# One wide matmul in place of two in a channel-major fp32 projection of a two-layer decoder trunk

## The chip, the core and the metric

The kernel runs on one core of a Trainium2 chip. The metric is device microseconds (us) of one execution; before the change the median of three runs is 497.79 us (497.72 to 498.26). A profiled execution gives the trace that is read below. PE is TensorE's matmul side, PEld its weight load, DVE VectorE, ACT ScalarE, POOL GpSimd, SP SyncE, which issues the weight loads.

## The reference

Two pre-norm residual layers over 256 tokens of 1024 channels, all in float32. Layer 0 mixes tokens by attention, layer 1 by causal pooling; each is followed by a squared-ReLU MLP of width 4096, and a last RMS norm ends the program. Cut to what matters here:

```python
# layer 0 (256 tokens are one block: plain causal attention, 8 heads of 128)
qkv = rms_norm(x, norm_mix[0]) @ w_qkv
q, k = rope(q), rope(k)                 # the first 32 channels of each head are rotated
x = x + softmax(causal(q @ k.T / sqrt(128))) @ v @ w_o
# both layers
h = relu(rms_norm(x, norm_mlp[l]) @ w_up[l])
x = x + (h * h) @ w_down[l]
```

## The kernel before

**Split operands.** A product of float32 values is made of products of float32r values. Each weight slab (1 MB: 128 partitions x 2048 elements) is loaded to a `raw` buffer by SP, ScalarE copies it to a high part `wh` (L160), and VectorE subtracts to get the low part `wl` (L164), in two pieces of 128x1024 (four for the first slabs). Activations are split likewise: `xs[:, k, 0:256]` is the high part of channel tile `k`, `xs[:, k, 256:512]` the low part. A product takes three passes, high x high, low weight x high, high weight x low.

**Channel-major products** (queries, keys, up-projection): the weights stand still, the activations move, and the result has channels on partitions and 256 tokens on the free axis. `chan_block` (L368) computes one half `f` (128 channels) of a slab: for each of eight channel tiles `k` three matmuls of 256 columns, at L360 (`wh` x high), L361 (`wl` x high) and L365 (`wh` x low). Both halves of a slab lie in one PSUM bank `u`, from a pool of two (`ps_u`), so a slab takes 48 matmuls. **Token-major products** (values, output projection, down-projection) move the weights and take three matmuls of 512 columns (L351 to L353).

**Order.** All engines run an order written out by hand: each executes its instructions in the order in which the code issues them. `pump(n)` issues the next n pieces of the weight split (a `wh` on ScalarE, a `wl` on VectorE), at most three slabs (`AHEAD`) ahead of the slab in use; `pump_h` and `pump_l` issue the halves of a piece apart. The split's last `wl` piece of a slab also issues a later slab's load on SP.

**Queries and keys** (loop at L571): for each of four head pairs `j`, the key slab, then the scores of the pair before, then the query slab, then the transposes of the probabilities of the pair before. `qk_evac` (L495) turns a bank into rotated keys or queries: VectorE shuffles 32 rows to `sw` (L500) and multiplies the bank by a cosine table into the tile `t` (L501); POOL multiplies `sw` by a sine table (L502) and adds it to `t` (L503). `scores` (L510) takes `t_k` and `t_q`: score matmuls into `s` (L517, L518), row maxima on VectorE (L521, negated at L525), exponentials with their sums on ScalarE (L530), reciprocal of the sums (L533) and scaling of the probabilities `p` (L537) on VectorE. `prob_t` transposes `p` on TensorE (L548).

**MLP** (`mlp`, L667): per step `i`, the up slab `u_i`, then the down slab of step `i - 2`; steps 0 to 2 have no down slab in front, so three up slabs stand in a row. `up_evac` (L641): ScalarE takes relu out of the bank (L646), VectorE squares it to `hf` (L647), ScalarE squares it to the high part `hh` (L648), VectorE subtracts to `hl` (L649). `first_up` (L652) computes slab 0 of a layer with the last transposes of the residual (`tr_m`, L287) in the middle of it; ScalarE (L293) and VectorE (L299) make the two parts of `xs` from them.

Of the kernel before, what the change touches and what calls it, by code (L numbers as in the profile page):

```python
# [83 lines left out]
def tile_trunk(ctx: ExitStack, tc: tile.TileContext, x_in, positions, norm_mix, norm_mlp,  # L84
# [237 lines left out]
    def rsqrt_steps(acc, s, nm):  # L322
        """1 / sqrt(variance + eps), in three steps: VectorE, ScalarE, VectorE."""
# [25 lines left out]
    def tok_mm(acc, lh, ll, wh, wl, first, last):  # L349
        """Three passes of a token-major product: hi*hi + hi*lo + lo*hi."""  # L350
# [4 lines left out]
    def chan_hi(acc, w, k, f, first):  # L355
        """Channel-major product with the activations' high part: two of the three passes."""
# [15 lines left out]

    def d_banks(nm):
# [18 lines left out]
    def rotary():  # L392
        """Angles reduced to one turn."""
# [83 lines left out]
    # rstd along the free axis, folded with the rotary tables  # L477
# [32 lines left out]
    def scores(j):  # L510
# [60 lines left out]
    for j in range(4):  # L571
        w = use("k", j)
        u = qk_bank("k", j)
        chan_block(u, w, 0)
# [8 lines left out]
        chan_block(u, w, 1)  # L583
# [3 lines left out]
        qk["k", j] = qk_evac("k", j, u)  # L587
# [53 lines left out]
    def up_evac(l, i, u):  # L641
        r = work.tile([P, HALF], F32, tag="Z", name="relu_%d_%d" % (l, i), bufs=4)
# [292 lines left out]
```

## Time and profile before

| what | value |
|---|---|
| median of three runs | 497.79 us |
| profiled execution, first to last instruction | 496.7 us |
| PE busy | 485.3 us (98%) |
| PEld busy | 442.2 us (89%) |
| DVE busy | 304.7 us (61%) |
| ACT busy | 245.7 us (49%) |
| POOL busy | 50.1 us (10%) |
| granted TensorE clock, mean | 0.996 |

The profiled execution's own time is its span, 496.7 us; the runs' median lies 1.1 us above it, which is what stands around the first and the last instruction. Busy times of an engine count each instruction from start to end, and matmuls overlap: the pace of TensorE is read from the starts of matmuls that follow each other, not from their durations.

### The profile page before, as it was taken

How to read it: one execution, taken by the hardware profiler on the slowest of the kernel's cores; microseconds unless marked ns; L12 is line 12 of the kernel's file. 1: busy time of each engine (PE TensorE's matmuls, PEld its weight loads, DVE VectorE, ACT ScalarE, POOL GpSimd, SP SyncE). 2: the span in 40 equal slices, each digit the busy share in tenths (PEclk: the TensorE clock that was granted, in tenths of full speed). 3: DMA queues.
4: the chain of work that ended last, by engine and by line, in shares of the span. 5: the costliest groups of instructions: out<-in, count | busy, mean ns of one | idle time of the engine just before them, and what ended most of it. 6: DMA issues, size and time to landing. Idle time of an engine off the chain costs nothing.

```text
span 496.7 us, 7616 instructions
## 1 busy us (share of the span) xinstructions
PE 485.3 (98%) x3137; PEld 442.2 (89%) x3137; DVE 304.7 (61%) x420; ACT 245.7 (49%) x363; POOL 50.1 (10%) x46
## 2 busy tenths in 40 slices
PE   9999999999999999999999999999999999999993
PEld 7789899889999999999999989999999999999982
DVE  3788788765858555555565576676455555544435
ACT  4776444554766444444444443584444444444423
POOL 6936524200000000000000000000000000000000
PEclk9999999999999999999999999999999999999998
DMA  7959525570596556555444660188555555666002
GB/s 269 385 167 282 167 87 169 157 246 22 180 360 192 193 203 211 207 194 170 170 170 173 187 234 1 52 260 295 192 177 170 169 172 184 200 204 230 29 0 84
DMA packets 56081, 89.59 MB, mean 180 GB/s; under 512 B 1600, under 2 KB 44640, under 8 KB 56048
## 3 DMA queue, kind: packets, MB, share of 16 engines
q1 hardware_dynamic: 55632, 88.68, 53.2%
q8 instruction: 24, 0.39, 0.3%
q10 hardware_dynamic: 352, 0.41, 0.2%
q14 instruction: 9, 0.07, 0.0%
q0 software_dynamic: 64, 0.03, 0.0%
HBM read 88.06 MB, written 1.05 MB: 179 GB/s over the span
## 4 chain that ended last, share of the span: by engine, by line
PE 88%; POOL 5%; DVE 2%; issue 2%; ACT 1%; DMA 1%; POOLq 0%; DVEq 0%; ACTq 0%
PE u_m L365 12%; PE u_m L361 12%; PE u_m L360 12%; PE d_m L353 12%; PE d_m L352 12%; PE d_m L351 12%; POOL rot_b L403 2%; PE d_o L353 1%; PE d_o L351 1%; PE d_o L352 1%; PE u_q L365 1%; PE u_q L360 1%; PE u_q L361 1%; PE pb L781 1%; DMA raw_k<-in_attn_w_qkv_dram 1%
## 5 line engine op out<-in xcount | busy, mean ns | idle before, releaser
L361 PE MATMUL u_m<-xs,wl_u 128*128 128x256 f32 x512 | 144.1, 283 | 0.0
L360 PE MATMUL u_m<-xs,wh_u 128*128 128x256 f32 x512 | 143.0, 281 | 0.0
L365 PE MATMUL u_m<-xs,wh_u 128*128 128x256 f32 x512 | 141.9, 285 | 0.0
L353 PE MATMUL d_m<-wh_d,hl 128*128 128x512 f32 x256 | 100.1, 391 | 0.0
L352 PE MATMUL d_m<-wl_d,hh 128*128 128x512 f32 x256 | 100.1, 391 | 0.0
L351 PE MATMUL d_m<-wh_d,hh 128*128 128x512 f32 x256 | 99.8, 390 | 0.0
L360 PEld LDWEIGHTS u_m<-xs,wh_u 128*128 128x128 f32 x512 | 97.0, 189 | 1.0
L361 PEld LDWEIGHTS u_m<-xs,wl_u 128*128 128x128 f32 x512 | 96.3, 188 | 1.0
L646 ACT ACTIVATE relu<-u_m 128x512 f32<-128x512 f32 x32 | 19.1, 597 | 157.2 <-PE u_m L365 157.2
L647 DVE TENSOR_TENSOR hf<-relu 128x512 f32<-128x512 f32 x32 | 22.1, 692 | 121.1 <-ACT relu L646 121.1
L365 PEld LDWEIGHTS u_m<-xs,wh_u 128*128 128x128 f32 x512 | 95.0, 189 | 0.0
L164 DVE TENSOR_TENSOR wl_d<-raw_d,wh_d 128x1024 fp32r<-128x1024 f32 x64 | 77.6, 1222 | 8.6 <-ACT wh_d L160 5.0
L164 DVE TENSOR_TENSOR wl_u<-raw_u,wh_u 128x1024 fp32r<-128x1024 f32 x64 | 75.3, 1219 | 1.7 <-ACT wh_u L160 1.5
L160 ACT ACTIVATE wh_d<-raw_d 128x1024 fp32r<-128x1024 f32 x64 | 66.1, 1045 | 6.7 <-DMA raw_d<-in_mlp_w_down_dram 6.7
L160 ACT ACTIVATE wh_u<-raw_u 128x1024 fp32r<-128x1024 f32 x64 | 63.7, 1045 | 0.0
L353 PEld LDWEIGHTS d_m<-wh_d,hl 128*128 128x128 f32 x256 | 48.0, 188 | 10.1
L352 PEld LDWEIGHTS d_m<-wl_d,hh 128*128 128x128 f32 x256 | 48.0, 188 | 9.5
L351 PEld LDWEIGHTS d_m<-wh_d,hh 128*128 128x128 f32 x256 | 48.1, 188 | 9.3
L649 DVE TENSOR_TENSOR hl<-hf,hh 128x512 fp32r<-128x512 f32 x32 | 22.2, 693 | 3.3
L648 ACT ACTIVATE hh<-relu 128x512 fp32r<-128x512 f32 x32 | 20.3, 634 | 1.1
L360 PE MATMUL u_q<-xs,wh_q 128*128 128x256 f32 x64 | 18.6, 290 | 0.0
L360 PE MATMUL u_k<-xs,wh_k 128*128 128x256 f32 x64 | 18.4, 288 | 0.0
(171 smaller groups left out, 595.2 us busy)
## 6 DMA issues: line engine op xcount, KB each, us to landing
raw_u<-in_mlp_w_up_dram SPq DMA_DIRECT2D x32, 1024.0 KB, 5.7
raw_d<-in_mlp_w_down_dram SPq DMA_DIRECT2D x32, 1024.0 KB, 6.7
raw_k<-in_attn_w_qkv_dram SPq DMA_DIRECT2D x4, 1024.0 KB, 5.4
raw_q<-in_attn_w_qkv_dram SPq DMA_DIRECT2D x4, 1024.0 KB, 5.3
raw_o<-in_attn_w_o_dram SPq DMA_DIRECT2D x4, 1024.0 KB, 5.1
raw_v<-in_attn_w_qkv_dram SPq DMA_DIRECT2D x3, 1024.0 KB, 9.7
raw_v<-in_attn_w_qkv_dram SPq DMA_DIRECT2D x4, 256.0 KB, 4.1
pw<-in_pool_w_dram SPq DMA_DIRECT2D x1, 1024.0 KB, 10.9
```

The source lines that it names most:

```text
L160: nc.scalar.activation(wh[:, sl], src[:, sl], AF.Copy)
L164: nc.vector.tensor_tensor(wl[:, sl], src[:, sl], wh[:, sl].bitcast(F32), op=ALU.subtract)
L351: nc.tensor.matmul(acc, lh, wh, start=first, stop=False)
L352: nc.tensor.matmul(acc, lh, wl, start=False, stop=False)
L353: nc.tensor.matmul(acc, ll, wh, start=False, stop=last)
L360: nc.tensor.matmul(o, w[0][:, k, fs], hi, start=first, stop=False, skip_group_check=True)
L361: nc.tensor.matmul(o, w[1][:, k, fs], hi, start=False, stop=False, skip_group_check=True)
L365: nc.tensor.matmul(acc[:, f * SEQ:(f + 1) * SEQ], w[0][:, k, fs], xs[:, k, SEQ:2 * SEQ], start=False, stop=last, skip_group_check=True)
L646: nc.scalar.activation(r, u, AF.Relu)
L647: nc.vector.tensor_tensor(hf, r, r, op=ALU.mult)
L648: nc.scalar.activation(hh, r, AF.Square)
L649: nc.vector.tensor_tensor(hl, hf, hh.bitcast(F32), op=ALU.subtract)
```

## The change

Three edits.

1. In the up-projection and in queries and keys, the high weights meet both activation parts in one matmul of 512 columns, since the two parts lie side by side in `xs`. Per `k` and `f` there are now two matmuls: `wl` x high (256 columns, L377 of the changed kernel) and `wh` x high and low (512 columns, L379), in this order. The result fills a whole bank per half slab: columns 0 to 255 hold two passes, columns 256 to 511 the third.
2. The two parts of the bank are added afterwards: ScalarE copies columns 256 to 511 to a tile `t`, VectorE adds columns 0 to 255 to it, for each half (L518 and L519 for queries and keys, L670 and L671 for the MLP). Rotation and squared ReLU then start from `t` in SBUF instead of the bank: `hf` is max(t, 0) x t in one VectorE instruction (L680), and `hh` a copy of `hf` on ScalarE (L681). For `j` = 0 the banks of queries and keys come from `ps_u`, for later pairs from the four banks (`ps_d`) that hold the values' sums before.
3. The scaling of the probabilities moves from VectorE (L537) to ScalarE (L564).

```diff
+    def wide_k(acc, w, k, f, first, last):
+        fs = slice(f * P, (f + 1) * P)
+        nc.tensor.matmul(acc[:, 0:SEQ], w[1][:, k, fs], xs[:, k, 0:SEQ],
+                         start=first, stop=False, skip_group_check=True)
+        nc.tensor.matmul(acc, w[0][:, k, fs], xs[:, k, :],
+                         start=False, stop=last, skip_group_check=True)
+
+    def wide_block(acc, w, f):
+        for k in range(KT):
+            wide_k(acc, w, k, f, k == 0, k == KT - 1)
+
+    def wide_bank(nm, i, f):
+        return ps_u.tile([P, HALF], F32, tag="u", name="u_%s_%d_%d" % (nm, i, f))
...
+    def qk_wide(nm, j, w, f, t):
+        if j == 0:
+            u = wide_bank(nm, j, f)
+        else:
+            u = ps_d.tile([P, HALF], F32, tag="d%d%d" % ("kq".index(nm), f), name="u_%s_%d_%d" % (nm, j, f))
+        wide_block(u, w, f)
+        nc.scalar.activation(t[:, f, :], u[:, SEQ:2 * SEQ], AF.Copy)
+        nc.vector.tensor_tensor(t[:, f, :], u[:, 0:SEQ], t[:, f, :], op=ALU.add)
...
-        nc.vector.stream_shuffle(sw.rearrange("p f t -> p (f t)"), u[0:ROT, :], swap)
-        nc.vector.tensor_tensor(t, uv, ct.broadcast_to([P, 2, SEQ]), op=ALU.mult)
+        nc.vector.stream_shuffle(sw.rearrange("p f t -> p (f t)"), t[0:ROT].rearrange("p f t -> p (f t)"), swap)
+        nc.vector.tensor_tensor(t, t, ct.broadcast_to([P, 2, SEQ]), op=ALU.mult)
...
-                nc.vector.tensor_scalar(pr[a][:, c0:c1], pr[a][:, c0:c1], sums[:, i:i + 1], None,
-                                        op0=ALU.mult)
+                nc.scalar.activation(pr[a][:, c0:c1], pr[a][:, c0:c1], AF.Copy, scale=sums[:, i:i + 1])
...
     for j in range(4):
         w = use("k", j)
-        u = qk_bank("k", j)
-        chan_block(u, w, 0)
+        t = qk_tile("k", j)
+        qk_wide("k", j, w, 0, t)
...
+    def up_sum(t, u, f):
+        ts = slice(f * SEQ, (f + 1) * SEQ)
+        nc.scalar.activation(t[:, ts], u[:, SEQ:2 * SEQ], AF.Copy)
+        nc.vector.tensor_tensor(t[:, ts], u[:, 0:SEQ], t[:, ts], op=ALU.add)
...
-        nc.scalar.activation(r, u, AF.Relu)
-        nc.vector.tensor_tensor(hf, r, r, op=ALU.mult)
-        nc.scalar.activation(hh, r, AF.Square)
+        nc.vector.scalar_tensor_tensor(hf, t, 0.0, t, op0=ALU.max, op1=ALU.mult)
+        nc.scalar.activation(hh, hf, AF.Copy)
...
-        u = qk_bank(nm, 0)
+        us = [wide_bank(nm, 0, f) for f in range(2)]
         for k0 in range(0, KT, 2):
             for f in range(2):
                 for k in (k0, k0 + 1):
-                    chan_hi(u, w, k, f, k == 0 and f == 0)
+                    wide_k(us[f], w, k, f, k == 0, k == KT - 1)
+                if f == 0 and k0 < 4:
+                    ev = transposes(k0 + 4, gbase, nm)
             if k0 < 4:
-                both(transposes(k0 + 4, gbase, nm, upool=k0 == 0))
-            for f in range(2):
-                for k in (k0, k0 + 1):
-                    chan_lo(u, w, k, f, k == KT - 1)
-        return up_evac(l, 0, u)
+                both(ev)
+        t = up_tile(l, 0)
+        for f in range(2):
+            up_sum(t, us[f], f)
+        return up_evac(l, 0, t)
...
-                u = qk_bank("m%d" % l, i)
-                chan_block(u, w, 0)
+                t = up_tile(l, i)
+                u = wide_bank("m%d" % l, i, 0)
+                wide_block(u, w, 0)
+                up_sum(t, u, 0)
                 pump(1)
-                chan_block(u, w, 1)
-                hid[i] = up_evac(l, i, u)
+                u = wide_bank("m%d" % l, i, 1)
+                wide_block(u, w, 1)
+                up_sum(t, u, 1)
+                hid[i] = up_evac(l, i, t)
                 pump(2)
```

How this moves instructions, at the three places of which the prediction speaks.

VectorE at the first head pair, before: the shuffle (L500) and the product (L501) of the keys and of the queries, with pieces of the split (L164) between them.

```order
L164 TENSOR_TENSOR wl_q_373<-raw_q_282,wh_q_372 128x1024
L164 TENSOR_TENSOR wl_k_420<-raw_k_348,wh_k_419 128x1024
L500 STREAM_SHUFFLE sw_k_452<-u_k_390 32x512
L501 TENSOR_TENSOR t_k_451<-u_k_390,ct_k 128x512
L164 TENSOR_TENSOR wl_k_420<-raw_k_348,wh_k_419 128x1024
L164 TENSOR_TENSOR wl_q_462<-raw_q_353,wh_q_461 128x1024 x2
L500 STREAM_SHUFFLE sw_q_519<-u_q_465 32x512
```

And of the change, the same stretch: the additions (L519) stand between the pieces.

```order
L519 TENSOR_TENSOR t_k_390<-u_k_0_391,t_k_390 128x256
L164 TENSOR_TENSOR wl_q_373<-raw_q_282,wh_q_372 128x1024
L164 TENSOR_TENSOR wl_k_415<-raw_k_348,wh_k_414 128x1024
L519 TENSOR_TENSOR t_k_390<-u_k_1_420,t_k_390 128x256
L527 STREAM_SHUFFLE sw_k_441<-t_k_390 32x512
L528 TENSOR_TENSOR t_k_390<-t_k_390,ct_k 128x512
L164 TENSOR_TENSOR wl_k_415<-raw_k_348,wh_k_414 128x1024
L164 TENSOR_TENSOR wl_q_451<-raw_q_353,wh_q_450 128x1024
L519 TENSOR_TENSOR t_q_454<-u_q_0_455,t_q_454 128x256
L164 TENSOR_TENSOR wl_q_451<-raw_q_353,wh_q_450 128x1024
L519 TENSOR_TENSOR t_q_454<-u_q_1_478,t_q_454 128x256
L527 STREAM_SHUFFLE sw_q_497<-t_q_454 32x512
```

Four additions stand ahead of the queries' shuffle that were not there, and shuffle and product now read `t`, which the last addition writes.

TensorE at the first up slab of layer 1, before, behind the last transposes of the residual (`tr_d`): the passes with the activations' high part first, the four with the low part (L365) behind the transposes `tr_m`.

```order
L287 MATMUL tr_d_2980<-ident,xt 128x128 x4
L360 MATMUL u_m_0_2990<-xs,wh_u_0_2778 128x256
L361 MATMUL u_m_0_2990<-xs,wl_u_0_2779 128x256
...
L287 MATMUL tr_m_4_2999<-ident,xt 128x128 x4
L365 MATMUL u_m_0_2990<-xs,wh_u_0_2778 128x256 x4
```

And of the change:

```order
L287 MATMUL tr_d_2700<-ident,xt 128x128 x4
L377 MATMUL u_m_0_0_2710<-xs,wl_u_0_2499 128x256
L379 MATMUL u_m_0_0_2710<-xs,wh_u_0_2498 128x512
L377 MATMUL u_m_0_0_2710<-xs,wl_u_0_2499 128x256
L379 MATMUL u_m_0_0_2710<-xs,wh_u_0_2498 128x512
L287 MATMUL tr_m_4_2716<-ident,xt 128x128 x4
```

The second matmul of the slab already reads the low part of channel tile 0; before, eight matmuls and four transposes stood ahead of the first that did.

VectorE behind the first up slabs of layer 0, in the change (`t_0`, `t_1`, `t_2` belong to slabs 0, 1 and 2):

```order
L671 TENSOR_TENSOR t_0_1195<-u_m_0_0_1143,t_0_1195 128x256
L671 TENSOR_TENSOR t_0_1195<-u_m_0_1_1144,t_0_1195 128x256
L680 SCALAR_TENSOR_TENSOR hf_0_1200<-t_0_1195 128x512
L682 TENSOR_TENSOR hl_0_1202<-hf_0_1200,hh_0_1201 128x512
L164 TENSOR_TENSOR wl_u_2_1207<-raw_u_2_1033,wh_u_2_1206 128x1024 x2
L671 TENSOR_TENSOR t_1_1223<-u_m_1_0_1224,t_1_1223 128x256
L164 TENSOR_TENSOR wl_d_0_1244<-raw_d_0_1041,wh_d_0_1243 128x1024
```

Before, `hf`, `hl` and the same pieces stood there without the additions; the addition for the first half of slab 1 now stands behind two pieces of slab 2's split.

## Rows read from the trace of the kernel before

**Rows 1.** The page's head: the span, busy time of each engine with its share of the span and its instructions, and the chain that ended last, by engine.

```profile
span 496.7 us, 7616 instructions
PE 485.3 (98%) x3137; PEld 442.2 (89%) x3137; DVE 304.7 (61%) x420; ACT 245.7 (49%) x363; POOL 50.1 (10%) x46
PE 88%; POOL 5%; DVE 2%; issue 2%; ACT 1%; DMA 1%; POOLq 0%; DVEq 0%; ACTq 0%
```

**Rows 2.** The waits of PE, whole program: who waited for whom, us in total, times, longest.

```profile
PE s L517 <- POOL t_q L503: 1.3, 1, 1.3
PE warm_up L270 <- DVE warm L220: 1.1, 1, 1.1
PE d_v L439 <- ACT xs L293: 1.0, 1, 1.0
```

**Rows 3.** The timeline of PE over one MLP step: start (us), duration (us), engine, line, operation. A block of 48 up matmuls from 251.21, a block of 24 down matmuls from 256.97, the next up block from 262.45.

```profile
249.63 0.39 PE L353 MATMUL d_m<-wh_d,hl 128*128 128x512 f32 x1
...
251.21 0.28 PE L360 MATMUL u_m<-xs,wh_u 128*128 128x256 f32 x1
...
256.97 0.39 PE L351 MATMUL d_m<-wh_d,hh 128*128 128x512 f32 x1
...
259.73 0.39 PE L351 MATMUL d_m<-wh_d,hh 128*128 128x512 f32 x1
...
262.45 0.28 PE L360 MATMUL u_m<-xs,wh_u 128*128 128x256 f32 x1
```

**Rows 4.** Groups of instructions by line, operation and shape, whole program: busy us, mean ns of one, idle time before.

```profile
L164 DVE TENSOR_TENSOR wl_u<-raw_u,wh_u 128x1024 fp32r<-128x1024 f32 x64 | 75.3, 1219 | 1.7 <-ACT wh_u L160 1.5
L649 DVE TENSOR_TENSOR hl<-hf,hh 128x512 fp32r<-128x512 f32 x32 | 22.2, 693 | 3.3
L647 DVE TENSOR_TENSOR hf<-relu 128x512 f32<-128x512 f32 x32 | 22.1, 692 | 121.1 <-ACT relu L646 121.1
L486 DVE SCALAR_TENSOR_TENSOR ct_k<-rb,cos_t 128x256 f32<-128x256 f32 x1 | 0.4, 411 | 0.0
L160 ACT ACTIVATE wh_u<-raw_u 128x1024 fp32r<-128x1024 f32 x64 | 63.7, 1045 | 0.0
L648 ACT ACTIVATE hh<-relu 128x512 fp32r<-128x512 f32 x32 | 20.3, 634 | 1.1
L530 ACT ACTIVATE p<-p,mx 128x256 f32<-128x256 f32 x8 | 4.0, 495 | 0.0
L530 ACT ACTIVATE p<-p,mx 128x128 f32<-128x128 f32 x8 | 3.2, 394 | 18.0 <-DVE mx L525 18.0
```

**Rows 5.** The timeline of PE, DVE and ACT at the first up slabs of a layer: two rows of layer 1, then three of layer 0.

```profile
308.17 0.37 PE L360 MATMUL u_m<-xs,wh_u 128*128 128x256 f32 x1
308.62 1.65 DVE L299 SCALAR_TENSOR_TENSOR xs<-tr_d,gcol,xs 128x256 fp32r<-128x256 f32 x4
121.95 0.28 PE L360 MATMUL u_m<-xs,wh_u 128*128 128x256 f32 x1
122.21 0.60 ACT L646 ACTIVATE relu<-u_m 128x512 f32<-128x512 f32 x1 [2.54 <-PE u_m L365]
127.65 0.28 PE L360 MATMUL u_m<-xs,wh_u 128*128 128x256 f32 x1
```

**Rows 6.** The timeline of DVE, POOL and PE at the first head pair, and a POOL row of the second (59.04).

```profile
40.20 1.22 DVE L164 TENSOR_TENSOR wl_k<-raw_k,wh_k 128x1024 fp32r<-128x1024 f32 x1 [0.70 <-ACT wh_k L160]
41.34 3.44 DVE L164 TENSOR_TENSOR wl_q<-raw_q,wh_q 128x1024 fp32r<-128x1024 f32 x2
44.72 0.73 DVE L500 STREAM_SHUFFLE sw_q<-u_q 32x512 f32<-32x512 f32 x1
45.94 2.34 DVE L164 TENSOR_TENSOR wl_k<-raw_k,wh_k 128x1024 fp32r<-128x1024 f32 x2
45.53 3.90 POOL L502 TENSOR_TENSOR sw_q<-sw_q,st_q 32x512 f32<-32x512 f32 x1 [2.97 <-DVE sw_q L500]
49.50 1.26 POOL L503 TENSOR_TENSOR t_q<-t_q,sw_q 32x512 f32<-32x512 f32 x1
59.04 1.27 POOL L502 TENSOR_TENSOR sw_q<-sw_q,st_q 32x512 f32<-32x512 f32 x1 [5.70 <-DVE sw_q L500]
49.21 0.28 PE L365 MATMUL u_k<-xs,wh_k 128*128 128x256 f32 x1
50.82 0.38 PE L517 MATMUL s<-t_k,t_q 128*128 128x128 f32 x1 [1.33 <-POOL t_q L503]
```

**Rows 7.** The timeline of PE, DVE and POOL around the last key slab: POOL's addition to the third pair's queries, scores from 80.26, transposes from 87.27; and one DVE row of the first pair's scores (53.11).

```profile
53.11 0.27 DVE L525 TENSOR_SCALAR mx<-mx 128x4 f32<-128x4 f32 x1
75.74 2.14 POOL L503 TENSOR_TENSOR t_q<-t_q,sw_q 32x512 f32<-32x512 f32 x1
80.26 0.39 PE L517 MATMUL s<-t_k,t_q 128*128 128x128 f32 x2
82.73 1.27 POOL L503 TENSOR_TENSOR t_k<-t_k,sw_k 32x512 f32<-32x512 f32 x1
82.99 1.04 DVE L525 TENSOR_SCALAR mx<-mx 128x4 f32<-128x4 f32 x1
86.25 1.01 DVE L537 TENSOR_SCALAR p<-p,sums 128x128 f32<-128x128 f32 x4
87.27 0.27 PE L548 MATMUL pt<-ident,p 128*128 128x128 f32 x1
```

More of the change, by code (lines that the diff above doesn't have):

```diff
@@ L493, in qk_bank, with qk_tile, qk_evac @@
         return ps_u.tile([P, HALF], F32, tag="u", name="u_%s_%d" % (nm, j))
-    def qk_evac(nm, j, u):
+    def qk_wide(nm, j, w, f, t):
[6 more added lines that the diff above has]
+        nc.vector.tensor_tensor(t[:, f, :], u[:, 0:SEQ], t[:, f, :], op=ALU.add)
+    def qk_tile(nm, j):
+        return work.tile([P, 2, SEQ], F32, tag="X", name="t_%s_%d" % (nm, j), bufs=4)
+    def qk_evac(nm, j, t):
         ct, st = tab[nm]
-        t = work.tile([P, 2, SEQ], F32, tag="X", name="t_%s_%d" % (nm, j), bufs=4)
         sw = work.tile([ROT, 2, SEQ], F32, tag="sw", name="sw_%s_%d" % (nm, j), bufs=2)
-        uv = u.rearrange("p (f t) -> p f t", f=2)
-        nc.vector.stream_shuffle(sw.rearrange("p f t -> p (f t)"), u[0:ROT, :], swap)
-        nc.vector.tensor_tensor(t, uv, ct.broadcast_to([P, 2, SEQ]), op=ALU.mult)
+        nc.vector.stream_shuffle(sw.rearrange("p f t -> p (f t)"), t[0:ROT].rearrange("p f t -> p (f t)"), swap)
+        nc.vector.tensor_tensor(t, t, ct.broadcast_to([P, 2, SEQ]), op=ALU.mult)
         nc.gpsimd.tensor_tensor(sw, sw, st.broadcast_to([ROT, 2, SEQ]), op=ALU.mult)
@@ L582, in tile_trunk @@
             attend(j - 2)
-        chan_block(u, w, 1)
+        qk_wide("k", j, w, 1, t)
         if j == 0:
@@ L586, in tile_trunk @@
             v_evac(1, 1)
-        qk["k", j] = qk_evac("k", j, u)
+        qk["k", j] = qk_evac("k", j, t)
         if j >= 1:
@@ L592, in tile_trunk @@
         w = use("q", j)
-        u = qk_bank("q", j)
-        chan_block(u, w, 0)
+        t = qk_tile("q", j)
+        qk_wide("q", j, w, 0, t)
         pump(1)
-        chan_block(u, w, 1)
-        qk["q", j] = qk_evac("q", j, u)
+        qk_wide("q", j, w, 1, t)
+        qk["q", j] = qk_evac("q", j, t)
         if j >= 1:
@@ L639, in residual, with up_tile, up_evac @@
             nc.vector.scalar_tensor_tensor(xv, bank, sc, xv, op0=ALU.mult, op1=ALU.add)
-    def up_evac(l, i, u):
-        r = work.tile([P, HALF], F32, tag="Z", name="relu_%d_%d" % (l, i), bufs=4)
+    def up_sum(t, u, f):
+        ts = slice(f * SEQ, (f + 1) * SEQ)
+        nc.scalar.activation(t[:, ts], u[:, SEQ:2 * SEQ], AF.Copy)
+        nc.vector.tensor_tensor(t[:, ts], u[:, 0:SEQ], t[:, ts], op=ALU.add)
+    def up_tile(l, i):
+        return work.tile([P, HALF], F32, tag="Z", name="t_%d_%d" % (l, i), bufs=4)
+    def up_evac(l, i, t):
         hf = work.tile([P, HALF], F32, tag="Z", name="hf_%d_%d" % (l, i), bufs=4)
@@ L672, in mlp @@
                 w = use("u%d" % l, i)
-                u = qk_bank("m%d" % l, i)
-                chan_block(u, w, 0)
+                t = up_tile(l, i)
+                u = wide_bank("m%d" % l, i, 0)
+                wide_block(u, w, 0)
+                up_sum(t, u, 0)
                 pump(1)
-                chan_block(u, w, 1)
-                hid[i] = up_evac(l, i, u)
+                u = wide_bank("m%d" % l, i, 1)
+                wide_block(u, w, 1)
+                up_sum(t, u, 1)
+                hid[i] = up_evac(l, i, t)
                 pump(2)
```

## Prediction

> **What bounds it now.** I read the head of the page first [rows 1]: matmuls stand on TensorE for 98% of the span, and 88% of the chain that ended last is TensorE. The table of waits [rows 2] says how tight that is: in 496.7 us TensorE waits 3.4 us, in three places, and one of them, 1.3 us at the first scores for POOL's `t_q`, lies in the part that is changed. So a shorter pace of matmuls shortens the time one for one, as long as nobody else becomes late. The profiled span is 496.7 us and the median of the runs 497.79 us; I make the sum on the span and add the 1.1 us between them. A measurement of this kernel can tell about 0.2% (1.0 us) from no change.
>
> **The pace of matmuls** is in the timeline [rows 3]. From 251.21 to 256.97 stand 48 up matmuls of 256 columns: 120.0 ns each. From 256.97 to 262.45 stand 24 down matmuls of 512 columns: 228.3 ns each; the last 12 of them, from 259.73, take 226.7 ns each, and seven from 249.63 to 251.21 take 225.7. So twice the columns cost 108 ns more, and some 12 ns of each matmul do not depend on its columns. The clock is at the upper of its two levels (1.2 and 2.4 GHz) throughout, a mean of 0.996 granted.
>
> **Merged matmuls.** Two matmuls of 240.0 ns become one of 512 columns, 16 times per slab, in 32 up slabs and 8 slabs of queries and keys: 640 times. The new matmul holds still what an up matmul held, and moves 512 float32r columns as a down matmul does, so its price is between 225.7 and 228.3; I take 227.3, between the block's mean and its last 12. 640 x 12.7 ns = **8.1 us less** (640 x 11.7 = 7.5 to 640 x 14.3 = 9.2). The Trainium skill (TensorE: Matmul & The Clock Gate, Back-to-back issue gap) gives a fixed cost of 2.5 ns per matmul beside its columns; by that rule the merge would give 640 x 2.5 = 1.6 us. The trace disagrees with it, 120.0 and 228.3 ns against the rule's 109.2 and 215.8, and the measurement decides.
>
> **The steady MLP steps cost nothing.** Per step of 11.24 us [rows 3] VectorE had four split pieces of 1.22, `hf` 0.69 and `hl` 0.69: 6.3 us [rows 4]. Two additions of 128x256 out of the bank come on top; the nearest row is `ct_k`, 0.41: 7.1 us of 11.0. ScalarE loses relu (0.60, [rows 5]) and gets two copies of 128x256: `hh` takes 0.63 for 512 columns and 128 columns cost 0.10 (the two `p` rows), so 0.43; 0.40 is used below. VectorE's 121.1 us of idle time ahead of `hf` [rows 4] is the cover, and a step's hidden tile is used two steps later. Were the cover gone, VectorE would set a step only above 11.0 us. SP's loads follow the split's last pieces, which keep their order and their three slabs of lead.
>
> **The first slabs of each layer cost 2.3 us.** Three terms.
> - *Low part earlier.* In layer 1 the slab starts at 308.17, but `xs`'s low parts are made by VectorE from 308.62, four in 1.65 us [rows 5]: the first at about 309.1. The second matmul now needs it, at 308.3: 0.8 us. In layer 0 VectorE is ahead; nothing.
> - *Two banks at once.* The first slab ends with its halves 0.7 us apart (two `k` of 347 ns), and slab 1 takes the bank of half 0. It is free after the result's delay (121.95 to 122.21: 0.26), a copy (0.40) and an addition (0.41): 1.1 us, so TensorE waits 0.4, twice.
> - *Slabs in a row.* Slabs 0, 1, 2 have no down slab between: slab 1 starts at 121.95, slab 2 at 127.65 [rows 5]. Counted from 122.21, VectorE does two additions, `hf`, waits for `hh` (0.63), `hl`: 3.0; then two pieces of the split, the first held by ScalarE's 1.05: 5.6; then the addition for half 0 of slab 1: 6.0. TensorE wants that bank at 5.7: 0.35, twice.
> Sum 0.8 + 0.8 + 0.7 = 2.3 (0.8 if only the first is real, 3.0 if slabs 1 and 2 each wait half as long again).
>
> **Queries and keys cost 3.8 us.** Here the cover is thin.
> - *First scores.* VectorE's queue from 41.34 to the queries' shuffle at 44.72 has no gap [rows 6]. Four additions, 1.6 us, now stand ahead of that shuffle; the idle 0.70 at 40.20 takes up some: shuffle at 45.6, or at 47.5 if ScalarE's pieces, now queued behind copies that wait for TensorE, come late as well. Shuffle 0.73 and product 0.69 no longer overlap: 47.0. Then POOL's pair L502 and L503: alone 2 x 1.27 [rows 6], but 5.23 in this very place, from 45.53 to 50.76, because two split pieces ran beside it (3.90 instead of 1.27). I let POOL start behind the product, since that now has both operands in SBUF, as the split pieces have. The Trainium skill (SBUF — State Buffer, Who interferes with whom) states that a VectorE instruction with two SBUF inputs and a POOL instruction that reads SBUF exclude each other; no row shows it for this product, and without it the term is 0.7 smaller. `t_q` is ready at 49.5 (POOL alone) to 54.1 (late shuffle); I take the pair as measured here, 52.2. TensorE was done with the keys at 49.33 (49.21 and one pace); three slabs are 0.6 shorter, so it arrives at 48.7 and waits 3.5 where it waited 1.5: **2.0 more** (-0.7 to 3.9).
> - *Scaling by ScalarE, pairs 2 and 3.* Scores begin at 80.26, the scaled probabilities are there at 87.26 and the transposes start at 87.27 [rows 7]: no slack at all. Now a copy (0.40), an addition (0.41) and the lost overlap stand ahead of the maxima in VectorE's order: 0.9 later. The scaling was 1.01 on VectorE; on ScalarE the like exponentials are 0.39 and 0.50 [rows 4], four overlapped about 1.5: 0.5 later. TensorE arrives 0.2 earlier. It waits about 0.85 for the first head, and again 0.4 for the second: 1.3. If the stall of `mx` (1.04, against 0.27 alone, while POOL ran `t_k` [rows 7]) falls away with the new times, 0.5. I take 0.9, twice: **1.8**. The transposes behind the second key slab have 3.5 us of late scores in front, which hide it there; the last ones have the output projection's matmuls around them.
> VectorE's lighter load there (16 scalings gone) helps no wait that I can name, because the additions take as much.
>
> **Sum:** -8.1 + 2.3 + 3.8 = -2.0, a span of 494.7, with the 1.1 **495.8 us**. Ends: -9.2 + 0.8 + 0.3 = -8.1 (489.7), where 0.3 is -0.7 and twice 0.5; and -7.5 + 3.0 + 6.5 = +2.0 (499.8), where 6.5 is 3.9 and twice 1.3.
>
> **Rivals.**
> - *Everything is covered.* VectorE's order has more room than my chains, POOL gets its turn between pieces and the scaled probabilities arrive in time. For it: in the later pairs POOL's L502 takes 1.27 [rows 6]. Against it: 87.26 against 87.27. Then -8.1 + 0.8 + 0 is 490.5 us. 0.20.
> - *The waits cancel the gain.* The same mechanisms at their upper ends: -7.5 + 2.3 + 5.5 = +0.3, 498.1 us (5.5 is 3.2 and twice 1.15). For it: VectorE is without a gap for 5 us ahead of the first `t_q`. 0.16.
> - *Slower: POOL's rotation becomes the bound of every head pair.* `t_q` of the third pair is ready at 75.74 + 2.14 = 77.88, scores at 80.26: slack 2.4 [rows 7]. The copy and the addition take 0.9 of it and ScalarE's queue (the copy of half 1 stands behind the scalings and a piece) some 0.5; if POOL's L502 took 3.90 each time, 2.6 more, TensorE would wait 1.8 at each of three scores, which hides the waits for the probabilities: -2.0 + 5.4 - 1.8 = +1.6, 499.4 us; with L503 at 3.90 too, 504.8. It decides from about 1.6 us per pair on. Against it: only one row of the eight queries' rows on POOL was that long. 0.10.
> - *The merge saves little.* If a wide matmul with `xs` moving took nearly the 240.0 ns of the two that it replaces, the gain would be gone and the waits would stay: 2.3 + 3.8 = +6.1, 503.9 us. The down matmuls, 228.3 at most [rows 3], speak plainly against it. 0.02. By the rule of the Trainium skill above, which leaves a gain of 1.6, it would be 502.3 us.
> The forecast itself, from -4.5 to -1.0 on the median: 0.52.
>
> **Numbers.** Faster by over 0.2% is the forecast's case and the covered one: 0.72; within it the cancelled case: 0.16; slower the last two: 0.12. The range 490.3 to 499.0 leaves out the far side of the covered case and of the slower ones, together under 0.2.
>
> **What would show it.** An up block of 32 matmuls should run in 5.55 us instead of 5.76; PE waits should name `s` behind POOL `t_q` (some 3.5 us), `pt` behind ACT `p` (0.5 to 1.3 each), and about 0.4 us behind the additions L671 at slabs 1 and 2. I am wrong if a wide matmul takes more than 235 ns in the steady steps, if MLP steps exceed 11.1 us, or if the queries and keys wait for splits instead.

## Result: 502.21 us, 0.8% slower

The changed kernel takes 502.21 us (median of four runs, 501.54 to 502.83) against 498.02 us (497.72 to 498.56) for the kernel before on the same chip: a ratio of 1.0081, with a 95% interval of 1.0068 to 1.0095. The forecast was 495.8 us with a range that ended at 499.0; its sign was wrong too. The profiled execution has a span of 501.0 us, 4.3 us above the one before.

The head of the page after, answering to [rows 1]:

```profile
span 501.0 us, 6355 instructions
PE 484.1 (97%) x2497; PEld 409.8 (82%) x2497; DVE 338.7 (68%) x484; ACT 260.3 (52%) x427; POOL 54.6 (11%) x46
PE 77%; DVE 11%; ACT 6%; DMA 2%; issue 2%; POOLq 0%; POOL 0%; SPq 0%; DVEq 0%; ACTq 0%
```

Matmuls still cover 97% of the span, but the chain that ended last has left TensorE: 77% instead of 88%, and VectorE and ScalarE have 17% instead of 3%. The waits of PE, answering to [rows 2] (us in total, times, longest):

```profile
PE s L544 <- POOL t_q L530: 4.1, 4, 2.8
PE s L544 <- DVE al L593: 1.5, 2, 0.8
PE warm_up L270 <- DVE warm L220: 1.1, 1, 1.1
...
PE u_m L379 <- DVE xs L299: 0.6, 1, 0.6
PE u_m L377 <- DVE t L671: 0.5, 2, 0.2
```

TensorE used to wait for the queries once, 1.3 us; now scores wait six times, 5.6 us in all, for POOL's `t_q` and for VectorE's `al`.

Where the time went, stage by stage (from the starts of the first key matmul, the first `d_o`, the first `u_m`, the first `pb`, the first `u_m` of layer 1, and the end, in the two traces):

| stage | before | after | difference |
|---|---|---|---|
| up to the first key slab | 32.1 | 32.7 | +0.6 |
| queries, keys, attention | 55.7 | 60.7 | **+5.0** |
| output projection, first up slab's start | 27.5 | 28.2 | +0.7 |
| MLP of layer 0 | 179.8 | 178.4 | **-1.4** |
| pooling mixer | 13.0 | 13.1 | +0.1 |
| MLP of layer 1 | 188.5 | 187.9 | **-0.6** |

The first line isn't the change: that stage's code is the same, and it took 31.5 to 32.5 us in the ten traces below. The second line scatters too: with the attention of before, unchanged, it took 54.7 or 55.7 us in five traces, and the 1.0 us lies ahead of the first scores. So both halves of the sum missed. The MLPs gave 2.0 us where 4.2 were forecast (512 merges at 12.7 ns less 2.3 at the first slabs), and the attention took 5.7 where 2.2 were forecast (3.8 less 128 merges).

The steady MLP step, in the timeline of PE (start, duration), answers to [rows 3]:

```profile
256.54 0.28 PE L377 MATMUL u_m<-xs,wl_u 128*128 128x256 f32 x1
256.65 0.40 PE L379 MATMUL u_m<-xs,wh_u 128*128 128x512 f32 x1
...
262.15 0.40 PE L351 MATMUL d_m<-wh_d,hh 128*128 128x512 f32 x1
...
267.63 0.28 PE L377 MATMUL u_m<-xs,wl_u 128*128 128x256 f32 x1
```

The up block runs from 256.54 to 262.15, 5.61 us: 0.15 less than the 5.76 of before, not the 0.21 forecast. The down block takes 5.48, as before. A step is 11.09 us, and nothing of VectorE or ScalarE shows in it.

### The profile page after: what moved, and what is told of

The parts are those of the page before. It is cut to its first block, busy times and chain, and to the rows that moved or that the text cites. A ratio compares the mean times of both kernels' runs of the same rounds, so it can differ in the third digit from the quotient of the medians.

```text
span 501.0 us, 6355 instructions
## 1 busy us (share of the span) xinstructions
PE 484.1 (97%) x2497; PEld 409.8 (82%) x2497; DVE 338.7 (68%) x484; ACT 260.3 (52%) x427; POOL 54.6 (11%) x46
## 3 DMA queue, kind: packets, MB, share of 16 engines
HBM read 88.06 MB, written 1.05 MB: 178 GB/s over the span
## 4 chain that ended last, share of the span: by engine, by line
PE 77%; DVE 11%; ACT 6%; DMA 2%; issue 2%; POOLq 0%; POOL 0%; SPq 0%; DVEq 0%; ACTq 0%
PE u_m L379 24%; PE u_m L377 12%; PE d_m L351 11%; PE d_m L352 11%; PE d_m L353 11%; PE d_v L455 3%; DMA raw_v<-in_attn_w_qkv_dram 2%; DVE wl_k L164 2%; DVE wl_q L164 1%; ACT p L557 1%; PE d_o L353 1%; PE d_o L351 1%; PE d_o L352 1%; DVE wl_o L164 1%; ACT p L564 1%
## 5 line engine op out<-in xcount | busy, mean ns | idle before, releaser
L379 PE MATMUL u_m<-xs,wh_u 128*128 128x512 f32 x512 | 181.4, 394 | 0.6 <-DVE xs L299 0.6
L377 PE MATMUL u_m<-xs,wl_u 128*128 128x256 f32 x512 | 145.6, 284 | 0.5 <-DVE t L671 0.5
L379 PEld LDWEIGHTS u_m<-xs,wh_u 128*128 128x128 f32 x512 | 96.2, 188 | 22.5 <-DVE xs L299 0.8
L377 PEld LDWEIGHTS u_m<-xs,wl_u 128*128 128x128 f32 x512 | 96.2, 188 | 2.6 <-DVE t L671 1.6
L164 DVE TENSOR_TENSOR wl_d<-raw_d,wh_d 128x1024 fp32r<-128x1024 f32 x64 | 77.9, 1224 | 22.9 <-ACT wh_d L160 22.9
L670 ACT ACTIVATE t<-u_m 128x256 f32<-128x256 f32 x64 | 24.4, 382 | 111.0 <-PE u_m L379 110.9
L164 DVE TENSOR_TENSOR wl_u<-raw_u,wh_u 128x1024 fp32r<-128x1024 f32 x64 | 75.4, 1219 | 1.7 <-ACT wh_u L160 1.6
L671 DVE TENSOR_TENSOR t<-u_m,t 128x256 f32<-128x256 f32 x64 | 27.1, 423 | 57.9 <-ACT t L670 57.9
L681 ACT ACTIVATE hh<-hf 128x512 fp32r<-128x512 f32 x32 | 20.2, 632 | 45.8 <-DVE hf L680 45.8
L680 DVE SCALAR_TENSOR_TENSOR hf<-t 128x512 f32<-128x512 f32 x32 | 22.2, 692 | 1.1
L379 PE MATMUL u_k<-xs,wh_k 128*128 128x512 f32 x64 | 22.7, 393 | 0.0
L379 PE MATMUL u_q<-xs,wh_q 128*128 128x512 f32 x64 | 22.6, 393 | 0.0
L377 PE MATMUL u_q<-xs,wl_q 128*128 128x256 f32 x64 | 18.6, 291 | 0.0
```

Source lines behind the costliest of these rows:

```text
L164: nc.vector.tensor_tensor(wl[:, sl], src[:, sl], wh[:, sl].bitcast(F32), op=ALU.subtract)
L377: nc.tensor.matmul(acc[:, 0:SEQ], w[1][:, k, fs], xs[:, k, 0:SEQ], start=first, stop=False, skip_group_check=True)
L379: nc.tensor.matmul(acc, w[0][:, k, fs], xs[:, k, :], start=False, stop=last, skip_group_check=True)
L670: nc.scalar.activation(t[:, ts], u[:, SEQ:2 * SEQ], AF.Copy)
L671: nc.vector.tensor_tensor(t[:, ts], u[:, 0:SEQ], t[:, ts], op=ALU.add)
L680: nc.vector.scalar_tensor_tensor(hf, t, 0.0, t, op0=ALU.max, op1=ALU.mult)
```

## Experiments

Each is compared with the kernel before, run on the same chip beside it (medians from 497.27 to 497.81); gains and losses are differences to that median, unless said otherwise.

**MLP alone** (the change, with queries and keys as before):

```diff
 # loop over head pairs
-        qk_wide("k", j, w, 0, t)
+        chan_block(u, w, 0)
...
 # scores
-                nc.scalar.activation(pr[a][:, c0:c1], pr[a][:, c0:c1], AF.Copy, scale=sums[:, i:i + 1])
+                nc.vector.tensor_scalar(pr[a][:, c0:c1], pr[a][:, c0:c1], sums[:, i:i + 1], None, op0=ALU.mult)
```

> Wide matmuls in the MLP alone; queries, keys and scaling as before the change. If the loss lies in queries and keys alone, the stages from the first up slab on keep what they gain in the changed kernel (1.4 us in layer 0, 0.6 us in layer 1): 496.0, 2.1 below before. If the loss of the queries and keys also costs the MLP's start (splits that come late), more: 494 to 495.

Measured: 496.12 us (494.93 to 496.31) against 497.54, ratio 0.9964 (0.9951 to 0.9976); MLP stages 178.4 and 187.9 as in the change. This half pays, some 1.4 us.

**Queries and keys alone** (the MLP as before, the rest of the change kept):

```diff
 # up_evac, first_up, mlp: as before the change
-                wide_block(u, w, 0)
-                up_sum(t, u, 0)
+                chan_block(u, w, 0)
```

> Wide matmuls in queries and keys and scaling on ScalarE; the MLP as before the change. Both theories: the loss of 5.0 us in queries and keys and 0.7 in the output projection stays without the MLP's gain: 503.5 to 504.3. If the parts do not add up, the difference to the sum of the other runs shows it.

Measured: 504.25 us (503.5 to 504.76), ratio 1.0129 (1.0115 to 1.0143); queries and keys 60.7 us, output projection 28.2, as in the change. So this half costs 6.7 us. In the traces each half's stages have the length that they have in the change, within 0.1 us; the timed medians add up to 5.3, where the change itself measured 4.2.

**Scaling back on VectorE** (the change without its last edit):

```diff
 # scores
-                nc.scalar.activation(pr[a][:, c0:c1], pr[a][:, c0:c1], AF.Copy, scale=sums[:, i:i + 1])
+                nc.vector.tensor_scalar(pr[a][:, c0:c1], pr[a][:, c0:c1], sums[:, i:i + 1], None, op0=ALU.mult)
```

> The changed kernel with the scaling of the probabilities back on VectorE; the wide matmuls stay everywhere. Ring theory: in the changed kernel each head pair takes 16.3 us because ScalarE and VectorE pass work round in a ring, and the scaling on ScalarE (1.50) stands in it with the copy (0.27) and the split piece (0.96) queued behind it; back on VectorE about 1.0 plus 0.35 stand there instead, a pair falls to about 14.9 us, and three pairs give back about 4 us: 498. Lock theory: the pairs are bound by split pieces stretched to 2.3 us beside POOL, which stay: 501.5 to 502.2.

Measured: 499.25 us (499.06 to 499.95), ratio 1.0032 (1.002 to 1.0045); queries and keys 58.4 us. That is 1.7 us above the kernel before, where the change is 4.2 above it: the edit costs 2.5 us in the changed kernel. Neither expectation of the time held: it falls between them. The head pairs did what the ring theory said: the transposes of the four pairs start at 60.13, 74.63, 89.64 and 103.95, so 14.5, 15.0 and 14.3 us apart, against 14.7, 14.7 and 14.3 before and 16.8, 16.3 and 15.2 in the change. What is left of the loss in queries and keys stands ahead of the first of them. TensorE waits once, for the rotated queries of the first pair

```profile
PE s L544 <- POOL t_q L530: 2.8, 1, 2.8
```

so that the first scores stand 19.9 us behind the first key matmul instead of 18.7; and behind that wait its granted clock is 0.50, the lower of its two levels (1.2 and 2.4 GHz), for some 3 us. A stretch of 2 us (length, busy time of PE, PEld, DVE, ACT, POOL, granted clock, DMA share, GB/s):

```profile
52.00:54.00 2.00, 2.00 (x7) 1.74 (x8) 1.84 (x5) 0.00 (x0) 0.00 (x0) 0.50 0.04 14
```

From the first scores to the first transposes it takes 8.4 us (51.72 to 60.13) with no wait of TensorE in them; the same matmuls take 7.0 in the change, where the granted clock stays at 1.00.

**Scaling alone** (the kernel before, with that edit only):

```diff
 # scores of the kernel before
-                nc.vector.tensor_scalar(pr[a][:, c0:c1], pr[a][:, c0:c1], sums[:, i:i + 1], None, op0=ALU.mult)
+                nc.scalar.activation(pr[a][:, c0:c1], pr[a][:, c0:c1], AF.Copy, scale=sums[:, i:i + 1])
```

> The kernel before with one edit, the scaling on ScalarE. Prediction's step: at pairs 2 and 3 there is no slack, 0.5 to 1.3 us are lost at each, 499.0 to 500.6. Ring theory: without the additions VectorE has room, and what is lost is the 0.5 us by which the scaling is longer, at most twice: 498.0 to 499.0.

Measured: 498.59 us (498.23 to 499.58), ratio 1.0021 (1.0012 to 1.003): 1.05 us more, as the ring theory had it. The same edit costs less than half of what it costs beside the additions, so the two parts of the change are not independent. The chain of waits of the changed kernel says how. One period of it (start, duration, what), from one pair's exponentials to the next's:

```profile
73.24 1.88 ACT p L557 x8
...
75.35 1.50 ACT p L564 x4
76.85 0.27 ACT t_q L518
77.12 0.96 ACT wh_q L160
...
78.11 1.23 DVE wl_q L164
79.33 0.35 DVE t_q L519
...
79.80 0.73 DVE sw_q L527
...
81.16 2.32 DVE wl_o L164
83.48 0.33 DVE t_k L519
83.81 1.88 DVE wl_o L164
85.69 0.60 DVE al L593
...
86.76 0.73 DVE sw_k L527
...
87.52 0.69 DVE t_k L528
...
89.56 1.88 ACT p L557 x8
```

No TensorE row is in it: the loop from 73.24 to 89.56 closes over ScalarE and VectorE alone, 16.3 us, where TensorE had set the period of before, 14.67. Each instruction is short, and neither engine is full (over two periods, from 60.0 to 92.7, VectorE is busy for 25.6 of 32.7 us, ScalarE for 19.5); it is their order, each behind the other in its queue, that takes the time. The scaling (1.50) stands in ScalarE's queue ahead of the copy of `t_q`, whose bank TensorE has finished more than 3 us before, and of a `wh` piece that VectorE waits for.

**The rotation on VectorE** (the change, with POOL's two operations moved). The pieces of 2.32 and 1.88 us in that chain, 1.22 elsewhere, stand beside POOL's operations; so POOL was the first suspect.

```diff
-        nc.gpsimd.tensor_tensor(sw, sw, st.broadcast_to([ROT, 2, SEQ]), op=ALU.mult)
-        nc.gpsimd.tensor_tensor(t[0:ROT], t[0:ROT], sw, op=ALU.add)
+        nc.vector.tensor_tensor(sw, sw, st.broadcast_to([ROT, 2, SEQ]), op=ALU.mult)
+        nc.vector.tensor_tensor(t[0:ROT], t[0:ROT], sw, op=ALU.add)
```

> The change, with POOL's two rotary operations of each slab (L529, L530) moved to VectorE. Port theory: POOL and VectorE get in each other's way when both read SBUF, so the rotation takes 1.78 us an operation on POOL instead of 1.27, and VectorE's weight pieces beside it 2.31 and 1.88 instead of 1.2 and 1.0. Then the first scores come about 2.4 us sooner, each head pair's chain loses some 0.8 us (4.2 us of two stretched pieces become 2 x 0.6 of rotation and 2.2 of pieces), and the time is 496.8 to 498.5. Chain theory alone (VectorE and ScalarE have too many steps in a row in each head pair, and who does the rotation is no matter): 501 to 503, the queries and keys still 59 us or more.

Measured: 502.22 us (501.46 to 502.66), ratio 1.0086 (1.0071 to 1.0101), where the change has 1.0081: no difference. Queries and keys 61.9 us. The port theory falls as an account of the time, though what it says of the operations is right. The waits of PE in this kernel:

```profile
PE pt L574 <- ACT p L564: 3.6, 3, 2.4
...
PE s L544 <- DVE al L593: 0.8, 1, 0.8
```

and its chain of waits where the change's had the stretched pieces:

```profile
79.26 0.72 DVE sw_q L527 x2
80.01 0.69 DVE t_q L528
80.70 0.60 DVE sw_q L529
...
81.94 1.21 DVE wl_o L164
83.14 0.34 DVE t_k L519
83.48 1.13 DVE wl_o L164
```

The pieces are back at 1.21 and 1.13, and the scores do not wait for `t_q` any more (the first stand at 48.6 instead of 52.6). But what is won is spent in the same queue on the rotation itself, the period is 16.9 (72.81 to 89.69 between exponentials), no shorter than the change's 16.3, and the wait turns up at the transposes instead.

**No additions** (the change with the scaling on VectorE; the queries and keys leave out the low activation half: its columns are computed and not added):

```diff
-        nc.scalar.activation(t[:, f, :], u[:, SEQ:2 * SEQ], AF.Copy)
-        nc.vector.tensor_tensor(t[:, f, :], u[:, 0:SEQ], t[:, f, :], op=ALU.add)
...
-        nc.vector.stream_shuffle(sw..., t[0:ROT]..., swap)
-        nc.vector.tensor_tensor(t, t, ct.broadcast_to([P, 2, SEQ]), op=ALU.mult)
+        for f in range(2):
+            nc.vector.stream_shuffle(sw[:, f, :], us[nm, j, f][0:ROT, 0:SEQ], swap)
+        for f in range(2):
+            nc.vector.tensor_tensor(t[:, f, :], us[nm, j, f][:, 0:SEQ], ct[:, 0, :], op=ALU.mult)
```

> The change with the scaling on VectorE, in which the queries and keys leave out the low activation half: its columns are still computed, but the 16 copies and 16 additions are not made, and shuffle and product read the high halves from the two PSUM banks as before the change. Chain theory (the copies and additions, and the product out of SBUF, are the rest of the loss): the queries and keys fall from 58.4 us to 53.5 to 55.7, the time from 499.25 to 495.3 to 496.6. Rival (two banks for each slab, or the wide matmuls' order, hold TensorE up): 498.4 to 499.3.

Measured: 495.73 us (495.17 to 496.19) against 497.81, ratio 0.9954 (0.9941 to 0.9968); queries and keys 55.0 us, scores 14.5 us apart. Its chain, by engine, has TensorE back:

```profile
PE 85%; DVE 6%; POOL 4%; issue 2%; ACT 2%; POOLq 0%; ACTq 0%; DVEq 0%
```

So the wide matmuls do not hold the attention up, and the two banks do so once: TensorE waits 1.3 us at the first queries for `t_k` to be read out of its bank. The wide matmuls by themselves make a pair 0.2 us shorter than the 14.67 of before. The copies, the additions and the product moved to SBUF cost 3.8 us (from 2.1 below the kernel before to 1.7 above it). In the two traces the queries and keys differ by 3.4, nearly all of it at the first head pair: 1.4 from the first key matmul to the first scores (18.5 against 19.9), 1.5 from there to the first transposes (6.9 against 8.4, at a granted clock of 1.00 here and the fall shown above there), and 0.5 in the three pairs behind (43.3 against 43.8).

**Scaling later** (the change, all operations kept, ScalarE's four scalings issued behind the copy of the queries' first half):

```diff
 # scores: the scaling loop moves to scale_p(j)
 # loop over head pairs
         qk_wide("q", j, w, 0, t)
         pump(1)
+        if j >= 1:
+            scale_p(j - 1)
         qk_wide("q", j, w, 1, t)
```

> The change, with ScalarE's four scalings of a head pair issued later: behind the copy of the queries' first half and its weight piece, ahead of the queries' second half (for the last pair they stay behind the exponentials). Nothing is left out and no operation changes engine. Queue theory (the loss of the scaling edit, 3.0 us beside the additions and 1.05 without them, is the copy of t_q that stands behind 1.5 us of scaling in ScalarE's queue, with a weight piece behind it that VectorE waits for): the 16.31 us of a head pair fall by 0.8 to 1.5, the queries and keys to 57 to 59.2 us, the time to 498.0 to 500.3. Rival (it is ScalarE's added work, or VectorE's, wherever it stands): 501.5 to 502.8.

Measured: 500.82 us (500.33 to 501.53) against 497.27, ratio 1.0066 (1.0051 to 1.0081). That is 3.55 us above the kernel before, 0.6 less than the change, and the two intervals overlap: the times alone don't show a gain. The time is 0.5 above the queue theory's range; the stage, 60.5 us, is above it as well. In the chain TensorE's rows are back:

```profile
72.29 1.87 ACT p L557 x8
74.16 0.27 ACT t_q L518
...
75.37 1.39 ACT p L568 x4
76.80 0.44 PE pt L578 x2
```

From the first scores to the last pair's transposes it is 54.3 us (52.10 to 106.40), in the change 55.2 (52.63 to 107.87), with the scaling on VectorE 52.2 (51.72 to 103.95), before 50.7 (50.82 to 101.55). The clock falls in the first and the third of these traces and not in the change's, but with queries and keys alone, where it falls as well, the stretch is 55.2 too. So in the traces the place of the scalings in the queue makes 0.9 of the 3.0 us by which the edit lengthens this stretch, the smaller part. The rest was not taken apart; the waits of PE in this kernel now name the transposes behind the scalings (0.6 us).

**Grouped by halves** (wide matmuls in the MLP alone; eight narrow, then eight wide). This and the next ask for the missing 3.5 ns per merge.

```diff
-        for k in range(KT):
-            wide_k(acc, w, k, f, k == 0, k == KT - 1)
+        for k in range(KT):    # narrow
+            nc.tensor.matmul(acc[:, 0:SEQ], w[1][:, k, fs], xs[:, k, 0:SEQ], ...)
+        for k in range(KT):    # wide
+            nc.tensor.matmul(acc, w[0][:, k, fs], xs[:, k, :], ...)
```

> Wide matmuls in the MLP alone, with a half slab's 8 narrow matmuls first and its 8 wide ones after them. Alternation theory (a wide slot takes 230.5 ns because it stands between narrow ones; in a row it settles at 226.7): an up block falls from 5.61 to 5.55 us, the time by 1.5 to 2 us below 496.12, to 494.1 to 494.7. Rival (the operands set the pace, not the order; or the first wide ones after narrow ones always take some 231): 495.8 to 496.4.

Measured: 496.29 us (495.65 to 496.62), ratio 0.9967 (0.9954 to 0.9979), an up block of 5.63 us. Alternation is not the cause.

**Narrow first slabs** (MLP alone, and `first_up` as before the change):

```diff
 def first_up(l, gbase, nm):
-        us = [wide_bank(nm, 0, f) for f in range(2)]
+        u = qk_bank(nm, 0)
...
-                    wide_k(us[f], w, k, f, k == 0, k == KT - 1)
+                    chan_hi(u, w, k, f, k == 0 and f == 0)
...
+        r = work.tile([P, HALF], F32, tag="Z", name="t_%d_0" % l, bufs=4)
+        nc.scalar.activation(r, u, AF.Relu)
+        return up_evac(l, 0, r)
```

> Wide matmuls in the MLP alone, and each layer's first up slab narrow in one bank, as before the change. First-slab theory: the wait for the low part of layer 1 (0.86 + 0.11 us) goes, a bank wait of 0.4 goes in each layer, and 32 merges of 9.2 ns are given back (0.3 us): 494.4 to 495.4. Rival (the waits are only put off: the second slab waits for its bank behind the first one's evacuation just the same): 495.9 to 496.5.

Measured: 494.92 us (494.06 to 495.31) against 497.81, ratio 0.9939 (0.9927 to 0.9952): faster than both kernels, and 1.2 us under the MLP alone. Layer 1 is 1.1 us shorter (186.8), layer 0 only 0.1. The waits of PE in it have no `xs` row, but still

```profile
PE u_m L377 <- DVE t L661: 0.4, 2, 0.3
```

So the wait for the low part goes, as expected; the bank wait is only put off by one slab.

**Sixteen in a row** (as the last, with a slab's 16 narrow matmuls first and then its 16 wide ones, in two banks):

```diff
-                wide_block(u, w, 0)
...
-                wide_block(u, w, 1)
+                for f in range(2):     # narrow, both halves
+                    for k in range(KT): nc.tensor.matmul(us[f][:, 0:SEQ], w[1]..., xs[:, k, 0:SEQ], ...)
+                for f in range(2):     # wide, both halves
+                    for k in range(KT): nc.tensor.matmul(us[f], w[0]..., xs[:, k, :], ...)
```

> As e7_narrow_first, with a slab's 16 narrow matmuls in a row and then its 16 wide ones, in two banks. Length theory (a wide slot settles at 226.7 ns once enough of them stand in a row, as the down block's do after five to nine): the second eight wide ones take 227, the first 231, an up block 5.58 us, the time 0.6 to 1.0 us below e7_narrow_first, 493.9 to 494.4. Rival (these operands give 230 to 232 in any order): an up block 5.60 to 5.64, the time 494.7 to 495.5. Above 496 if two banks that come free together make the next slab wait.

Measured: 496.25 us (495.94 to 497.54) against 497.27, ratio 0.9981 (0.9971 to 0.999). The timeline of PE (16 matmuls folded into a row):

```profile
251.49 3.89 PE L706 MATMUL u_m<-xs,wh_u 128*128 128x512 f32 x16
255.21 0.39 PE L351 MATMUL d_m<-wh_d,hh 128*128 128x512 f32 x1
```

Sixteen wide ones take 3.72 us, 232.5 ns each: in a row they are no quicker than between narrow ones, and the length theory falls too. The time is above its rival's range too: by the ratios 2.1 us over the last kernel. The MLPs are 1.9 us longer (179.3 and 187.8), of which up blocks of 5.64 instead of 5.61 make 0.8. The other 1.0 lies at the start of each layer: from the last transposes inside slab 0 to the first down slab it takes 15.7 and 15.6 us where the last kernel takes 15.2 and 15.0, and TensorE waits 0.7 us for additions instead of 0.4. That fits what the expectation named last, two banks that come free together.

## Why the prediction was wrong

- **The pace of a wide matmul** was put at 227.3 ns, between 225.7 and 228.3, from the down block. It is some 231 ns: of a pair's 350.7 (5.61 us / 16) the narrow one takes 120.0. A merge saves some 9.2 ns, not 12.7, and 640 of them 5.9 us instead of 8.1. This step failed in its choice of rows. Those down matmuls move weights past a standing activation; the new one moves `xs` past standing weights. In the down block itself the last 12 run at 226.7 and those right behind an up block at some 231. Order does not explain the pace (232.5 in a row, 231 alternating); what does is open: the operands still differ, and they were not exchanged. By the rule of the Trainium skill (TensorE: Matmul & The Clock Gate, Back-to-back issue gap), which that section gives for an isolated matmul, a merge would give 2.5 ns; 9.2 lies well above it, so that sentence stands. That the prediction's sum by that rule, 502.3, comes so near to 502.21 is chance: the MLPs did gain, and the loss stands in the attention.
- **Steady MLP steps** were put at no cost: right. The step is shorter by 0.15 us, exactly the up block's gain, and the down block is unchanged.
- **First slabs**, 2.3 us: right in size. The MLPs gained 2.0 us, and 32 up slabs 0.147 less each are 4.7, so 2.7 went here. Of the three terms, the low part in layer 1 came near its price (0.87 for 0.8):

```profile
313.11 0.37 PE L377 MATMUL u_m<-xs,wl_u 128*128 128x256 f32 x1
314.10 0.50 PE L379 MATMUL u_m<-xs,wh_u 128*128 128x512 f32 x1 [0.62 <-DVE xs L299]
```

  The second matmul stands 0.99 us behind the first where 0.12 is the pace. Slab 1 waits 0.4 as priced, in both layers: between the starts

```profile
127.98 0.39 PE L379 MATMUL u_m<-xs,wh_u 128*128 128x512 f32 x1
128.60 0.39 PE L377 MATMUL u_m<-xs,wl_u 128*128 128x256 f32 x1 [0.23 <-DVE t L671]
```

  lie 0.62 instead of 0.23. Slab 2 has about 0.1 where 0.35 was put. No term was put for what follows a wait: there the next matmul takes 0.1 longer (at slab 1 to 128.82, 0.22 instead of 0.12), five times in all, about what slab 2 was priced too high.
- **First scores**, 2.0 us: near in size (1.6), in part by luck. `t_q` was forecast at 52.2 and TensorE's wait at 3.5, 2.8 in the trace:

```profile
48.59 1.78 POOL L529 TENSOR_TENSOR sw_q<-sw_q,st_q 32x512 f32<-32x512 f32 x1 [3.75 <-DVE sw_q L527]
49.16 2.30 DVE L164 TENSOR_TENSOR wl_k<-raw_k,wh_k 128x1024 fp32r<-128x1024 f32 x1
50.45 2.12 POOL L530 TENSOR_TENSOR t_q<-t_q,sw_q 32x512 f32<-32x512 f32 x1
52.63 0.49 PE L544 MATMUL s<-t_k,t_q 128*128 128x128 f32 x2 [2.82 <-POOL t_q L530]
```

  It was ready at 52.57, but by two errors that cancel: POOL started at 48.59 instead of 47.0 (the queries' shuffle at 47.77 was near the late case, and POOL followed it at once, beside the product and not behind it), and its pair took 4.0 us instead of 5.23. From the last key matmul (49.42) to the scores it is 3.2 us, 1.6 more than before (49.21 to 50.82, [rows 6]).
- **Scaling, pairs 2 and 3**, 1.8 us: the step that failed, in place and size. The wait was looked for at the transposes, which have no row in the waits of PE; it stands at the scores, pair after pair. And the pairs in between were put at nothing: "the transposes behind the second key slab have 3.5 us of late scores in front, which hide it there". They hid nothing, because a late start of the loop doesn't shorten its period: from the first scores to the last transposes it is 4.5 us more than before (55.2 against 50.7). I priced each engine's queue up to one wait and never added the loop up once around. Either edit alone leaves the pairs near TensorE's own pace, 14.3 to 15.0 us between transposes with the additions and 14.3 to 15.7 with the scaling; with both, the loop of ScalarE and VectorE takes 16.3 and is the bound.
- **VectorE's lighter load**, which was to help no wait because the additions take as much: right as load, and beside the point: the load isn't the bound.
- **The slower rival** (POOL's rotation the bound of every head pair, 499.4 to 504.8) has the time and the place. Its cause was not the one: L529 took 1.79 us and not 3.90, and with the rotation on VectorE the time is the same. The half sentence in it about the copy "behind the scalings and a piece" points at what the later scaling confirmed in part.

In short, in steps from the kernel before: wide matmuls everywhere, with the additions in queries and keys left out and the scaling on VectorE, gain 2.1 us (1.4 of it with the MLP alone). The copies, additions and the product in SBUF lose 3.8 (shown by leaving them out), mostly once, at the first head pair: a longer wait and TensorE's lower clock behind it. The scaling on ScalarE loses 2.5 more (shown by moving it back), and this in every pair, because with both edits ScalarE and VectorE set the period. Of that loss the place of the scalings in ScalarE's queue explains 0.9 of 3.0 in the traces; how the rest divides stays open. The steps add up to the change's 4.2 because each starts where the one before ends.

## What to carry to other kernels

Where TensorE sits in a loop with other engines' in-order queues, add up that loop once around, with every instruction that stands ahead in each queue, and compare it with TensorE's own period; slack at each single wait doesn't show that the loop fits. An edit that is cheap alone (1.05 us here) can cost more than twice as much (2.5) beside another that lengthens the same loop, so apply such edits apart. And price a single long wait of TensorE with what may follow it: here the lower clock behind 2.8 us cost another 1.4 where TensorE was the bound. The version worth keeping has the wide matmuls in the MLP alone with narrow first slabs: 494.92 us, 0.6% under the kernel before.

## What was not expected of the hardware

**After the same wait the clock falls in one execution and not in another.** In the kernel with queries and keys alone, whose attention is that of the change, TensorE stands still for 2.8 us ahead of the first scores, as in the change. Stretches of 2 us (length, busy time of PE, PEld, DVE, ACT, POOL, granted clock, DMA share, GB/s), first that kernel, then the change:

```profile
50.00:52.00 2.00, 0.00 (x0) 0.00 (x0) 2.00 (x3) 1.06 (x1) 2.00 (x1) 0.95 0.70 240
52.00:54.00 2.00, 1.89 (x7) 1.71 (x8) 1.88 (x4) 0.00 (x0) 0.06 (x1) 0.50 0.01 4
54.00:56.00 2.00, 2.00 (x9) 1.74 (x9) 1.97 (x9) 0.00 (x0) 1.59 (x1) 0.69 0.85 240
```

```profile
50.00:52.00 2.00, 0.00 (x0) 0.00 (x0) 2.00 (x3) 1.29 (x2) 1.92 (x2) 1.00 0.98 337
52.00:54.00 2.00, 1.37 (x9) 1.29 (x9) 2.00 (x2) 0.00 (x0) 0.58 (x1) 1.00 0.03 10
```

In the first the granted clock is 0.50 from 52 to 54, the lower of the two levels (1.2 of 2.4 GHz); in the second it stays at 1.00. From the first scores to the first transposes that makes 8.5 us (52.11 to 60.63) against 7.0 (52.63 to 59.66). Yet at the last transposes both have taken 55.2 us (to 107.34 and 107.87): the slower matmuls are hidden, since the loop is set by ScalarE and VectorE. Other traces with a wait of 2.8 us there show the fall too (scaling on VectorE, later scaling), where TensorE is nearer to being the bound. With the scaling on VectorE the chain of waits runs over TensorE's rows alone from the first scores (51.72) to 67.9, so there the 8.4 us up to the first transposes, instead of 7.0, count in full.

**POOL and VectorE stretch each other when both read SBUF.** POOL's L529 takes 1.79 us on average in the change, where the like row was 1.27 [rows 6], since the product `t` beside it reads SBUF and no longer PSUM; a VectorE piece beside POOL's operations takes 2.30 instead of 1.22 [rows 4]. The Trainium skill (SBUF — State Buffer, Who interferes with whom) states the exclusion, and the trace agrees. It makes single operations late. With POOL's work moved to VectorE the pieces were short again and the time was the same; what the stretch alone costs was not measured, since the rotation then stood in VectorE's queue.
